# Where in a 256-byte block the operands of 17,664 matmuls begin: one offset for all activations, one for high weights, one for low weights

## The chip, the cores and the metric

The kernel runs on one core of a Trainium2 chip. The metric is the device time of one execution in microseconds (us); three runs of the kernel before took 2746.3, 2747.49 and 2748.06 us, so the median is 2747.49 us. Engines are called PE (TensorE), DVE (VectorE), ACT (ScalarE), POOL (GpSimd) and SP (SyncE).

## What is computed

One inference step of a decoder with two layers, on 256 prompt positions and 8 x 8 sample positions, 320 columns in all, with 2048 features. Layer 0 mixes tokens by gated linear attention, layer 1 by a gated MLP over chunks of 128 positions; each is followed by a dense MLP with a squared ReLU, and after each of the four there is a residual with a layer norm:

```python
for i in range(DEPTH):                       # DEPTH = 2, D_MODEL = 2048, D_FF = 8192
    if i % N_MIXERS == 0:
        h, s = gla_mixer(x, gla_w_in[j], gla_w_gate[j], gla_b_gate[j], gla_norm_g[j],
                         gla_w_out[j], gla_state0[j])
    else:
        h, v_rows = sg_mixer(x, sg_w_in[j], sg_b_in[j], ..., sg_w_out[j])
    x = layer_norm(DEEPNORM_ALPHA * x + h, ln1_g[i], ln1_b[i])
    x = layer_norm(DEEPNORM_ALPHA * x + sq_relu_mlp(x, mlp_w1[i], mlp_w2[i]), ln2_g[i], ln2_b[i])

def sq_relu_mlp(x, w1, w2):
    return jnp.square(jax.nn.relu(x @ w1)) @ w2
```

All inputs are float32. Nearly all of the work is the products with the weight matrices, some 400 MB that are read once.

## The kernel before

Features lie on the 128 partitions and positions along the free axis, so that an activation is 16 k tiles (`KT`) of 128 x 320 floats, 1280 bytes a tile and partition. Each float32 product is made of three products of a shorter float type (`F32R`): an activation is kept as a high part and a low part (`xh`, `xl`; `yh`, `yl`; `hh`, `hl`; `oh`, `ol`; `ph`, `pl`; `dgh`, `dgl`), and so are the weights (`wh`, `wl`).

**A unit.** `unit` (L117) loads one block of weights, 4 k tiles by 256 columns, 512 KB, from SP's queue into a `raw` buffer (three deep); ACT copies it to `wh` (L128), which rounds it, and DVE subtracts to get `wl` (L129). `group` (L143) then runs over the unit's two halves of 128 output features and its four k tiles, and `mm3` (L136) issues three matmuls, a triple, for each: 24 matmuls a unit.

```python
nc.tensor.matmul(ps, wl[:, kk, s], x_h, start=first, stop=False)
nc.tensor.matmul(ps, wh[:, kk, s], x_l, start=False, stop=False)
nc.tensor.matmul(ps, wh[:, kk, s], x_h, start=False, stop=last)
```

The weights are the stationary operand and the activations stream. PE loads the weights of the next matmul while the current one streams, so that a triple has these pairs side by side: `x_h` streams beside the load of `wh`, `x_l` beside a second load of the same `wh`, `x_h` beside the load of the next `wl`.

**The rings.** `wh` and `wl` have four buffers each in the pool `wa` (ring a). From the last part of the output projection of layer 0 on there is a second pool `wb` of the same size (ring b), and units alternate between the two (`next_ring`, L132). An order of the instructions is made by the tile framework's scheduler.

**The activations.** `bigtile` (L176) makes a tile of 16 x 322 floats; `TW` is 322 because a product of un-normed activations (`dgh`, `dgl`, `gemm_of`) has two more columns. `starts` puts an activation some floats further into its tile: `mlp` (L784) uses `8 * c` for chunk c of its four chunks, in layer 0 for both parts, in layer 1 for the low part alone, and `gemm_of` 32 for the high part of `y` in layer 1. One chunk of an MLP is 32 units on `y` (first product) and 32 units on `h` (second product); the first chunk's first product begins with 8 units of 322 columns.

The addresses of the built program, modulo 256 bytes, are these. A k tile is five blocks of 256 bytes (1280) long, and a step of `wh` or `wl` 512 or 1024 bytes, so that the offset is one for all 320-column matmuls of a tile. With 322 columns the step is 1288 bytes and the offset moves on by 8.

| stretch, us from the start | activations | high part at | low part at |
|---|---|---|---|
| to 1355, `x`, `o`, `y` of layer 0 | most units | 32 | 160 |
| 679.70 to 792.23, `h` chunk 0, layer 0 | 32 units | 32 | 160 |
| 904.76 to 1017.71, `h` chunk 1, layer 0 | 32 units | 64 | 192 |
| 1130.25 to 1242.67, `h` chunk 2, layer 0 | 32 units | 96 | 224 |
| 1355.20 to 1467.70, `h` chunk 3, layer 0 | 32 units | 128 | 0 |
| 1496 to 1824, `y`, `p` of the gated MLP | most units | 32 | 160 |
| 2049.88 to 2162.52 and other `y` chunks, layer 1 | 32 units each | 160 | 160 |
| 2162.52 to 2274.52, `h` chunk 1, layer 1 | 32 units | 32 | 192 |
| 2387.16 to 2499.90, `h` chunk 2, layer 1 | 32 units | 32 | 224 |
| 2612.54 on, `h` chunk 3, layer 1 | 32 units | 32 | 0 |

Weights of ring a begin at 160, high and low; those of ring b at 224, high and low.

**The heads.** In layer 0 the attention of head h is interleaved with the projections of the next (`Head.steps`). `sample_o` squares the sample outputs into `sq` (L571), a buffer of its own, and DVE reduces it to `s1` (L573), of which PE forms a sum (L576). `ev_k` of the next head writes two tiles `kend` (L371 and L372) in the ring `vfm`, two buffers of 1024 bytes, which PE transposes (L382).

Of the kernel before, what the change touches and what calls it, by code (L numbers as in the profile page):

```python
# [8 lines left out]
F32 = mybir.dt.float32  # L9
F32R = mybir.dt.float32r  # L10
# [5 lines left out]
P = 128  # L16
D = 2048
KT = D // P
TP = 256
DB, DS = 8, 8  # L20
T = TP + DB * DS
TW = T + 2
# [8 lines left out]
UK = 4  # L31
UN = 256
NU = KT // UK


V_BG, V_NG = 0, 8
# [5 lines left out]
class Ring:  # L42


    def __init__(self, pool, tag):
        self.pool, self.tag = pool, tag


class Side:
# [17 lines left out]
def step_kernel(ctx: ExitStack, tc: tile.TileContext, A):  # L67
# [3 lines left out]
    def nm(s):  # L71
        uid[0] += 1
        return f"{s}_{uid[0]}"


    cp = ctx.enter_context(tc.tile_pool(name="cp", bufs=1))
# [32 lines left out]
    nc.vector.memset(eps_l[:], LN_EPS)  # L109
    eps_h = cp.tile([P, 1], F32, tag="epsh", name="eps_h")  # L110
    nc.vector.memset(eps_h[:], HEAD_EPS)

    def col(c):
        return vec[:, c : c + 1]
# [2 lines left out]
    def unit(w, row0, q, col0, ring):  # L117

        raw = wraw.tile([P, UK, UN], F32, tag="raw", name=nm("raw"))
        src = w[row0 // (UK * P) + q, col0 // UN]  # L120
        hi = ring.pool.tile([P, UK, UN], F32R, tag="h" + ring.tag, name=nm("wh"))
        lo = ring.pool.tile([P, UK, UN], F32R, tag="l" + ring.tag, name=nm("wl"))
        units[0] += 1
        step = 2 if units[0] <= 2 else UK
        for k in range(0, UK, step):
            ks = slice(k, k + step)
            nc.sync.dma_start(raw[:, ks, :], src[:, ks, :])
            nc.scalar.copy(hi[:, ks, :], raw[:, ks, :])  # L128
            nc.vector.tensor_sub(lo[:, ks, :], raw[:, ks, :], hi[:, ks, :].bitcast(F32))  # L129
        return hi, lo  # L130
# [42 lines left out]
    w_in = A["gla_w_in"]  # L173
    C_Q, C_K, C_V, C_R = 0, H * DK, 2 * H * DK, 2 * H * DK + H * DV

    def bigtile(tag, dt, name, width=T, start=0):  # L176

        t = (lp if tag == "b1" else big).tile([P, KT * TW], dt, tag=tag, name=nm(name))
        return t[:, start : start + KT * width].rearrange("p (k t) -> p k t", t=width)

    def parts(pair, name, width=T, starts=(0, 0)):
        return (bigtile(pair + "0", F32R, name + "h", width, starts[0]),
                bigtile(pair + "1", F32R, name + "l", width, starts[1]))

    xh, xl = parts("a", "x")
    o_all = bigtile("b0", F32, "o_all")
# [106 lines left out]
    class Head:  # L293
# [266 lines left out]
        def sample_o(hd):  # L560
            h, s1 = hd.h, hd.s1
            os_ = gp.tile([P, DV], F32, tag="sq", name=nm("os"))
            nc.scalar.copy(os_[:], hd.po[:])
            pt = gltile()
            for vt in range(4):
                nc.tensor.transpose(pt[:, vt * P : (vt + 1) * P], os_[:, vt * P : (vt + 1) * P], ident[:])
            pv = pt[:].rearrange("p (v c t) -> p v c t", v=4, c=2)
            o_s = o_all[:, 4 * h : 4 * h + 4, TP:T]
            nc.scalar.copy(o_s, pv[:, :, 0, :])
            nc.vector.tensor_add(o_s, o_s, pv[:, :, 1, :])  # L570
            sq = gp.tile([P, 4, DB * DS], F32, tag="sqs", name=nm("sq"))  # L571
            nc.scalar.activation(sq[:], o_s, AF.Square)
            nc.vector.tensor_reduce(s1[:, TP:T], sq[:].rearrange("p v t -> p t v"), axis=AX.X, op=ALU.add)  # L573

            pr = gltile(T)
            nc.tensor.matmul(pr[:], ones[:], s1[:], start=True, stop=True)  # L576
            hd.rs = gp.tile([P, T], F32, tag="rs", name=nm("rs"))
            rsqrt(hd.rs[:], pr[:], 1.0 / DV, HEAD_EPS, eps_h, gp)
# [33 lines left out]
    def second_half():  # L612

        nonlocal lp, l2, z, gl, mx
        side.flush()
        split_o(range(4 * (H - 1), 4 * H))
        gst.close()
        gls.close()
        gl = ctx.enter_context(tc.tile_pool(name="gs", bufs=2, space=bass.MemoryType.PSUM))
        mx = ctx.enter_context(tc.tile_pool(name="mx", bufs=2, space=bass.MemoryType.PSUM))  # L620
        banks[0] = 3
        lp = ctx.enter_context(tc.tile_pool(name="lp", bufs=1))
        l2 = ctx.enter_context(tc.tile_pool(name="l2", bufs=2))
        wb = ctx.enter_context(tc.tile_pool(name="wb", bufs=4))
        rings.append(Ring(wb, "b"))
        z = lp.tile([P, KT, T], F32, tag="z", name="z")
        for q in range(2):
            nc.gpsimd.dma_start(z[:, 8 * q : 8 * q + 8, :], xT[:, 8 * q : 8 * q + 8, :])

# [118 lines left out]
                  lambda n, ps, i=i: evict(2 * i + n, ps), side, before=before if i == 0 else None)  # L748
            i += n2

    def gemm_of(norm, out, w, col0, evict_raw, evict, starts=(0, 0)):

        yh, yl = parts(out, "y", starts=starts)
        norm.close()
        side = Side([lambda j=j: norm.apply(j, yh, yl) for j in range(KT)], 3 * NU)
        group(w, 0, (col0, col0 + UN), *norm.raw, evict_raw, side, width=TW)
        side.flush()
        for i in range(2, D // UN):
            group(w, 0, (col0 + i * UN,), yh, yl, lambda n, ps, i=i: evict(2 * i + n, ps))
        return yh, yl  # L760
# [23 lines left out]
    def mlp(i, norm, y_in, h_in, vg, vb, raw, last=False):  # L784

        w1, w2 = A["mlp_w1"][i], A["mlp_w2"][i]
        NC_ = 4
        for c in range(NC_):
            hs = []

            def sq_relu(j, x, r):
                if not hs:
                    hs.extend(parts(h_in, "h", starts=(8 * c, 8 * c) if i == 0 else (0, 8 * c)))
                hh, hl = hs
                f = l2.tile([P, T], F32, tag="f", name=nm("f"))
                nc.vector.scalar_tensor_tensor(f[:], x, 0.0, r[:], op0=ALU.max, op1=ALU.mult)
                nc.scalar.copy(hh[:, j, 0:T], f[:])
                nc.vector.tensor_sub(hl[:, j, 0:T], f[:], hh[:, j, 0:T].bitcast(F32))

            def evict(j, ps):  # L800
                r = l2.tile([P, T], F32, tag="r", name=nm("r"))
                nc.scalar.activation(r[:], ps[:], AF.Relu)  # L802
                sq_relu(j, ps[:], r)

            def evict_raw(j, ps):
                t, wb_ = norm.correct(ps)
                r = l2.tile([P, T], F32, tag="r", name=nm("r"))
                nc.scalar.activation(r[:], t[:], AF.Relu, bias=wb_)
                sq_relu(j, r[:], r)

            if c == 0:
                yh, yl = gemm_of(norm, y_in, w1, 0, evict_raw, evict, starts=(0, 0) if i == 0 else (32, 0))
            else:
                gemm(w1, 0, c * D, yh, yl, evict)
            if c < NC_ - 1:
                def evz(j, ps, s=ALPHA if c == 0 else 1.0):
                    nc.vector.scalar_tensor_tensor(z[:, j, :], z[:, j, :], s, ps[:], op0=ALU.mult, op1=ALU.add)
                gemm(w2, c * D, 0, *hs, evz)
            else:
                return residual_gemm(w2, *hs, c * D, 1.0, vg, vb, raw, last=last)  # L820
# [209 lines left out]
```

## Time and profile before

| | us |
|---|---|
| median of three runs | 2747.49 |
| the profiled execution | 2747.28 |
| its span, first to last instruction | 2745.6 |
| PE matmul busy | 2726.5 |
| DVE busy | 1544.6 |
| ACT busy | 1182.2 |

The busy time of PE says little about its pace, since matmuls overlap and their ends are modelled: 309 ns is the mean of one, while a new one starts every 147 ns or so. So a stretch is read here by its length and the work in it: windows of the trace begin and end at the start of the first matmul of a unit. A window counts one to three matmuls more than its own, those still under way at its edges.

### The profile page before, as it was taken

The page shows a single profiled execution, that of the slowest core. Times are in us where ns is not written, and L with a number is a line of the kernel's source. Part 1 is how long each engine was busy: PE and PEld are TensorE (multiplying, and loading weights), DVE is VectorE, ACT ScalarE, POOL GpSimd, SP SyncE. Part 2 cuts the span into 40 slices and gives each one's busy share as a digit, 9 for nine tenths or more (in the row PEclk, how much of TensorE's full clock was granted, in tenths as well). Part 3 has the DMA queues.
Part 4 walks back from the last instruction along what each step waited for, and adds up shares of the span by engine and source line. Part 5 has one row for each costly group of instructions (what it writes and reads, how often), then busy time and mean ns, then how long its engine had stood idle before and what let it go on. Part 6 is the DMA issues. An engine that isn't in the chain of part 4 may idle for free.

```text
span 2745.6 us, 44621 instructions
## 1 busy us (share of the span) xinstructions
PE 2726.5 (99%) x18493; PEld 2703.0 (98%) x18493; DVE 1544.6 (56%) x2284; ACT 1182.2 (43%) x1698; POOL 54.4 (2%) x84
## 2 busy tenths in 40 slices
PE   8999999999999999999999999999999999999998
PEld 8999999999999999999999999999999999999998
DVE  6577577885444434444468774686444444444446
ACT  5545455464334334323345554455334333323433
POOL 1000000000000000000001000000000000000001
PEclk9999999999999999999999999999999999999999
DMA  6557566644444444444445444454444444444442
GB/s 224 178 191 237 163 209 212 208 145 154 152 148 153 147 150 150 152 148 150 150 146 169 148 138 130 141 160 154 147 153 147 153 149 151 149 151 149 151 148 75
DMA packets 126395, 434.51 MB, mean 158 GB/s; under 512 B 13680, under 2 KB 17904, under 8 KB 126192
## 3 DMA queue, kind: packets, MB, share of 16 engines
q1 hardware_dynamic: 118800, 407.29, 47.4%
q0 software_dynamic: 6512, 23.20, 2.4%
q8 instruction: 144, 2.36, 0.4%
q10 hardware_dynamic: 880, 1.18, 0.1%
q14 instruction: 59, 0.48, 0.1%
HBM read 409.60 MB, written 22.02 MB: 157 GB/s over the span
## 4 chain that ended last, share of the span: by engine, by line
PE 98%; DVE 1%; ACT 1%; DMA 0%; issue 0%; SPq 0%; ACTq 0%; DVEq 0%
PE mm L139 31%; PE mm L141 31%; PE mm L140 31%; PE gl L551 1%; PE gl L554 1%; PE gl L509 1%; DMA xr<-xT 0%; PE gl L889 0%; PE gl L493 0%; ACT z L963 0%; PE gl L884 0%; PE gl L494 0%; PE gl L418 0%; PE gl L420 0%; PE gl L472 0%
## 5 line engine op out<-in xcount | busy, mean ns | idle before, releaser
L129 DVE TENSOR_TENSOR wl<-raw,wh 128x1024 fp32r<-128x1024 f32 (+1 forms) x738 | 900.9, 1222 | 966.2 <-ACT wh L128 963.7
L128 ACT CAST wh<-raw 128x1024 fp32r<-128x1024 f32 (+1 forms) x738 | 771.0, 1046 | 1235.4 <-PE mm L141 1120.1
L141 PE MATMUL mm<-yh,wh 128*128 128x320 f32 x2368 | 730.9, 309 | 0.0
L140 PE MATMUL mm<-yl,wh 128*128 128x320 f32 x2368 | 728.5, 308 | 0.0
L139 PE MATMUL mm<-yh,wl 128*128 128x320 f32 x2368 | 725.5, 309 | 0.0
L141 PE MATMUL mm<-hh,wh 128*128 128x320 f32 x2048 | 632.2, 309 | 0.0
L139 PE MATMUL mm<-hh,wl 128*128 128x320 f32 x2048 | 631.8, 309 | 0.0
L140 PE MATMUL mm<-hl,wh 128*128 128x320 f32 x2048 | 631.4, 308 | 0.0
L140 PEld LDWEIGHTS mm<-yl,wh 128*128 128x128 f32 x2368 | 444.8, 188 | 0.0
L141 PEld LDWEIGHTS mm<-yh,wh 128*128 128x128 f32 x2368 | 444.0, 188 | 0.0
L139 PEld LDWEIGHTS mm<-yh,wl 128*128 128x128 f32 x2368 | 443.0, 188 | 0.0
L139 PEld LDWEIGHTS mm<-hh,wl 128*128 128x128 f32 x2048 | 385.0, 188 | 0.0
L140 PEld LDWEIGHTS mm<-hl,wh 128*128 128x128 f32 x2048 | 384.5, 188 | 0.0
L141 PEld LDWEIGHTS mm<-hh,wh 128*128 128x128 f32 x2048 | 384.3, 188 | 0.0
L139 PE MATMUL mm<-xh,wl 128*128 128x320 f32 x768 | 242.1, 316 | 8.7 <-ACT xh L202 5.6
L140 PE MATMUL mm<-xl,wh 128*128 128x320 f32 x768 | 240.8, 314 | 0.0
L141 PE MATMUL mm<-xh,wh 128*128 128x320 f32 x768 | 239.2, 311 | 0.0
L139 PEld LDWEIGHTS mm<-xh,wl 128*128 128x128 f32 x768 | 145.8, 190 | 13.6 <-ACT xh L202 5.6
L140 PEld LDWEIGHTS mm<-xl,wh 128*128 128x128 f32 x768 | 145.8, 190 | 3.5 <-issue 1.2
L141 PEld LDWEIGHTS mm<-xh,wh 128*128 128x128 f32 x768 | 145.9, 190 | 1.3
L139 PE MATMUL mm<-ph,wl 128*128 128x320 f32 x256 | 78.6, 309 | 1.0 <-ACT ph L922 1.0
L802 ACT ACTIVATE r<-mm 128x320 f32<-128x320 f32 x120 | 52.5, 438 | 62.1 <-PE mm L141 62.1
(271 smaller groups left out, 2490.2 us busy)
## 6 DMA issues: line engine op xcount, KB each, us to landing
raw<-mlp_w SPq DMA_DIRECT2D x512, 512.0 KB, 3.5
raw<-gla_w_in SPq DMA_DIRECT2D x94, 512.0 KB, 3.8
raw<-sg_w_in SPq DMA_DIRECT2D x64, 512.0 KB, 3.6
st<-state SPq DMA_DIRECT2D x32, 512.0 KB, 4.2
o_state_s<-st POOLq DMA_DIRECT2D x32, 512.0 KB, 4.1
raw<-gla_w_out SPq DMA_DIRECT2D x32, 512.0 KB, 3.7
raw<-sg_w_out SPq DMA_DIRECT2D x32, 512.0 KB, 3.6
z<-xT POOLq DMA_DIRECT2D x2, 1280.0 KB, 11.3
```

What stands on the lines that cost most here:

```text
L128: nc.scalar.copy(hi[:, ks, :], raw[:, ks, :])
L129: nc.vector.tensor_sub(lo[:, ks, :], raw[:, ks, :], hi[:, ks, :].bitcast(F32))
L139: nc.tensor.matmul(ps, wl[:, kk, s], x_h, start=first, stop=False)
L140: nc.tensor.matmul(ps, wh[:, kk, s], x_l, start=False, stop=False)
L141: nc.tensor.matmul(ps, wh[:, kk, s], x_h, start=False, stop=last)
L509: nc.tensor.matmul(pu[:], hd.ktp[:, blk, kt * P : (kt + 1) * P], hd.vtp[:, blk, :], start=(blk == 0), stop=(blk == 1))
L551: nc.tensor.matmul(po[:], qm[:, kt, b * P : (b + 1) * P], part[:], start=False, stop=(b == DB - 1 and kt == 1 and part is sth))
L554: nc.tensor.matmul(pu[:], kz[:, g, i, kt * P : (kt + 1) * P], hd.vts[:, g, :], start=True, stop=True)
L802: nc.scalar.activation(r[:], ps[:], AF.Relu)
```

## The change

All tiles of activations grow to `BIG` = 16 x 320 + 64 floats, a multiple of 256 bytes, and begin at a multiple of 256. Activations of 320 columns begin 32 floats (128 bytes) into the tile, those of 322 columns at its beginning; `starts` is gone. Padding tiles (`fill`, `gap`, `fill_b`, `fill_l`), which no instruction uses, shift what follows them: `wh` begins at 0 in both rings, and since `gap` lies between the high and the low buffers, `wl` begins at 64 in both. To make room `sq` of `sample_o` moves into the ring `vfm`. In the built program every main matmul of 320 columns has its activations at 128, `wh` at 0 and `wl` at 64.

```diff
+LINE = 64
+BIG = KT * T + LINE
...
-        self.pool, self.tag = pool, tag
+        self.pool, self.tag, self.gap = pool, tag, False
+
+    def part(self, p, name):
+
+        t = self.pool.tile([P, UK, UN], F32R, tag=p + self.tag, name=name)
+        if not self.gap:
+            self.pool.tile([P, LINE // 4], F32, tag="gap", name=name + "_gap", bufs=1)
+            self.gap = True
+        return t
...
+    cp.tile([P, LINE - 8], F32, tag="fill", name="fill")
...
-        hi = ring.pool.tile([P, UK, UN], F32R, tag="h" + ring.tag, name=nm("wh"))
-        lo = ring.pool.tile([P, UK, UN], F32R, tag="l" + ring.tag, name=nm("wl"))
+        hi = ring.part("h", nm("wh"))
+        lo = ring.part("l", nm("wl"))
...
-    def bigtile(tag, dt, name, width=T, start=0):
-
-        t = (lp if tag == "b1" else big).tile([P, KT * TW], dt, tag=tag, name=nm(name))
+    def bigtile(tag, dt, name, width=T):
+        t = (lp if tag == "b1" else big).tile([P, BIG], dt, tag=tag, name=nm(name))
+        start = LINE // 2 if width == T else 0
         return t[:, start : start + KT * width].rearrange("p (k t) -> p k t", t=width)
...
-            sq = gp.tile([P, 4, DB * DS], F32, tag="sqs", name=nm("sq"))
+            sq = g2.tile([P, 4, DB * DS], F32, tag="vfm", name=nm("sq"))
...
+        wb.tile([P, LINE // 4], F32, tag="fill", name="fill_b", bufs=1)
         z = lp.tile([P, KT, T], F32, tag="z", name="z")
+        lp.tile([P, 3 * LINE // 4], F32, tag="fill", name="fill_l")
...
-                    hs.extend(parts(h_in, "h", starts=(8 * c, 8 * c) if i == 0 else (0, 8 * c)))
+                    hs.extend(parts(h_in, "h"))
...
-                yh, yl = gemm_of(norm, y_in, w1, 0, evict_raw, evict, starts=(0, 0) if i == 0 else (32, 0))
+                yh, yl = gemm_of(norm, y_in, w1, 0, evict_raw, evict)
```

The instructions are the same in kind and number, and SP's and POOL's queues keep their order. DVE's, ACT's and PE's change only around the place where a head ends and the next begins, three times.

DVE's queue there, before. `kend_1693` is the second of the next head, `s_132_1012` is `s1`, `sq_1583` the squares, `o_all` the outputs, which are weighted:

```order
L129 TENSOR_TENSOR wl_1782<-raw_1780,wh_1781 128x1024
L372 TENSOR_TENSOR kend_1693<-kte_1667,fac 128x256
L378 TENSOR_TENSOR kst_1695<-kte_1667,kst_1695 128x8x16
L397 SCALAR_TENSOR_TENSOR qd_1664<-mm_1278,eb_1311 128x320
L573 TENSOR_REDUCE s_132_1012<-sq_1583 128x64
```

The same place of DVE's queue after the change, where `kend_1677` is the first `kend` of the head, which stood six rows earlier, and `kend_1695` the second:

```order
L386 TENSOR_TENSOR kend_1677<-kte_1669,fac 128x256
L392 TENSOR_TENSOR kst_1697<-kte_1669,kst_1697 128x8x16
L411 SCALAR_TENSOR_TENSOR qd_1666<-mm_1280,eb_1313 128x320
L587 TENSOR_REDUCE s_132_1014<-sq_1585 128x64
L471 SCALAR_TENSOR_TENSOR o_all_91<-o_all_91,vec,sr_1075 128x320
L471 SCALAR_TENSOR_TENSOR o_all_91<-o_all_91,vec,sr_1077 128x320
L471 SCALAR_TENSOR_TENSOR o_all_91<-o_all_91,vec,sr_1274 128x320
L471 SCALAR_TENSOR_TENSOR o_all_91<-o_all_91,vec,sr_1276 128x320
L411 SCALAR_TENSOR_TENSOR qd_1666<-mm_1281,eb_1319 128x320
L414 TENSOR_TENSOR qx_1667<-qd_1666,fac 128x192
L414 TENSOR_TENSOR qx_1667<-qd_1666,fac 128x128
L386 TENSOR_TENSOR kend_1695<-kte_1669,fac 128x256
```

The second `kend` moved behind the reduction, four weightings and the two `qx`.

PE's queue at the same place, before; `mm_1718` is an output of the next projection, `ident` the matrix for transposes:

```order
L139 MATMUL mm_1718<-xh_88,wl_1752 128x320
L140 MATMUL mm_1718<-xl_89,wh_1751 128x320
L141 MATMUL mm_1718<-xh_88,wh_1751 128x320
L576 MATMUL gl_1586<-s_132_1012,ones 128x320
L382 MATMUL gl_1680<-ident,kend_1675 128x128 x2
L384 MATMUL gl_1680<-ident,kst_1677 128x128 x2
L382 MATMUL gl_1698<-ident,kend_1693 128x128 x2
L384 MATMUL gl_1698<-ident,kst_1695 128x128 x2
```

PE's queue after:

```order
L151 MATMUL mm_1720<-xl_90,wh_1753 128x320
L152 MATMUL mm_1720<-xh_89,wh_1753 128x320
L590 MATMUL gl_1588<-s_132_1014,ones 128x320
L396 MATMUL gl_1682<-ident,kend_1677 128x128 x2
L398 MATMUL gl_1682<-ident,kst_1679 128x128 x2
L150 MATMUL mm_1720<-xh_89,wl_1754 128x320
...
L152 MATMUL mm_1721<-xh_89,wh_1753 128x320
L396 MATMUL gl_1700<-ident,kend_1695 128x128 x2
L398 MATMUL gl_1700<-ident,kst_1697 128x128 x2
```

The sum over `s1` and the first transposes come one triple earlier among the main matmuls, and the second transposes some triples later.

## Rows read from the trace of the kernel before

**Rows 1.** The page: span, busy time with its share of each engine, granted clock.

```profile
span 2745.6 us, 44621 instructions
...
PE 2726.5 (99%) x18493; PEld 2703.0 (98%) x18493; DVE 1544.6 (56%) x2284; ACT 1182.2 (43%) x1698; POOL 54.4 (2%) x84
...
PEclk9999999999999999999999999999999999999999
```

**Rows 2.** Waits of PE: waiter <- releaser: us in all, times, longest us.

```profile
PE mm L139 <- ACT xh L202: 5.6, 1, 5.6
PE mm L139 <- DVE qd L397: 2.1, 1, 2.1
```

**Rows 3.** Groups: line, engine, op, count; busy us, mean ns; idle before, releasers.

```profile
L128 ACT CAST wh<-raw 128x1024 fp32r<-128x1024 f32 (+1 forms) x738 | 771.0, 1046 | 1235.4 <-PE mm L141 1120.1 <-issue 38.2 <-DMA raw<-gla_w_out 24.0
...
L141 PE MATMUL mm<-dgh,wh 128*128 128x322 f32 x192 | 59.6, 310 | 0.0
```

**Rows 4.** Windows of 32 units: from:to us, length, PE busy (matmuls), clock, DMA, GB/s.

```profile
679.70:792.23 112.53, 112.53 (x770) 1.00 0.48 150
904.76:1017.71 112.95, 112.95 (x770) 1.00 0.48 150
2049.88:2162.52 112.64, 112.64 (x771) 1.00 0.49 150
2162.52:2274.52 112.00, 112.00 (x771) 1.00 0.48 151
2387.16:2499.90 112.74, 112.74 (x770) 1.00 0.47 150
```

**Rows 5.** Windows of single units with weights of ring a.

```profile
823.88:827.40 3.52, 3.52 (x27) 1.00 0.49 156
2306.20:2309.72 3.52, 3.52 (x26) 1.00 0.42 151
2194.02:2197.52 3.50, 3.50 (x27) 1.00 0.47 151
2425.96:2429.44 3.48, 3.48 (x27) 1.00 0.37 148
2418.86:2422.38 3.52, 3.52 (x26) 1.00 0.47 149
2651.23:2654.75 3.52, 3.52 (x26) 1.00 0.51 150
2644.21:2647.72 3.51, 3.51 (x27) 1.00 0.45 149
1386.80:1390.30 3.50, 3.50 (x27) 1.00 0.50 154
```

**Rows 6.** Windows of single units with weights of ring b.

```profile
820.37:823.88 3.51, 3.51 (x27) 1.00 0.52 149
2302.68:2306.20 3.52, 3.52 (x26) 1.00 0.43 149
2190.52:2194.02 3.50, 3.50 (x27) 1.00 0.50 150
2422.38:2425.96 3.58, 3.58 (x27) 1.00 0.42 148
2415.34:2418.86 3.52, 3.52 (x26) 1.00 0.50 150
2647.72:2651.23 3.51, 3.51 (x26) 1.00 0.50 152
2640.68:2644.21 3.53, 3.53 (x27) 1.00 0.50 149
933.00:936.53 3.53, 3.53 (x26) 1.00 0.51 149
1158.35:1161.87 3.52, 3.52 (x26) 1.00 0.51 151
```

**Rows 7.** Timeline where a head ends: start us, length us, engine, line, operation.

```profile
155.86 0.61 DVE L573 TENSOR_REDUCE s<-sq 128x64 f32<-128x256 f32 x1
...
159.58 0.70 PE L576 MATMUL gl<-s,ones 128*128 128x320 f32 x2
```

More of the change, by code (lines that the diff above doesn't have):

```diff
@@ L174, in step_kernel, with parts @@
     C_Q, C_K, C_V, C_R = 0, H * DK, 2 * H * DK, 2 * H * DK + H * DV
-    def bigtile(tag, dt, name, width=T, start=0):
-        t = (lp if tag == "b1" else big).tile([P, KT * TW], dt, tag=tag, name=nm(name))
+    def bigtile(tag, dt, name, width=T):
+        t = (lp if tag == "b1" else big).tile([P, BIG], dt, tag=tag, name=nm(name))
+        start = LINE // 2 if width == T else 0
         return t[:, start : start + KT * width].rearrange("p (k t) -> p k t", t=width)
-    def parts(pair, name, width=T, starts=(0, 0)):
-        return (bigtile(pair + "0", F32R, name + "h", width, starts[0]),
-                bigtile(pair + "1", F32R, name + "l", width, starts[1]))
+    def parts(pair, name, width=T):
+        return bigtile(pair + "0", F32R, name + "h", width), bigtile(pair + "1", F32R, name + "l", width)
     xh, xl = parts("a", "x")
@@ L749, in gemm, with gemm_of @@
             i += n2
-    def gemm_of(norm, out, w, col0, evict_raw, evict, starts=(0, 0)):
-        yh, yl = parts(out, "y", starts=starts)
+    def gemm_of(norm, out, w, col0, evict_raw, evict):
+        yh, yl = parts(out, "y")
         norm.close()
```

## The prediction

> **What bounds the kernel now.** [...] Then the list of who waits for whom on PE [rows 2]: its longest entry is 5.6 us, once, at the start, and the second is 2.1 us, once. Nothing that ScalarE, VectorE or the DMA queues do in the main loops ends a wait of PE. So the time is the number of matmuls times the distance between their starts, and only what changes that distance can move it.
>
> The work comes in units: one unit is one 512 KB block of weights, split by one ScalarE copy, and 24 matmuls on it. The copy line counts 738 [rows 3]; the first two units copy in two halves, so there are 736 units. The matmuls of one of three products on 322 columns count 192 [rows 3], which is 24 units of 8; the other 712 units work on 320 columns. [...]
>
> [...] The blocks of [rows 4] do the same 768 matmuls at the same clock, and differ by 0.95 us. What differs is where the operands begin in a 256-byte block. I write hi/lo for the distance in bytes, modulo 256, by which the high and the low activations begin past the weights of that unit. [rows 5] has units of ring a, [rows 6] of ring b, in the order 32/160, 160/160, 32/192, 32/224 (two), 32/0 (two) of activation offsets, with 128/0 at the end of ring a and 64/192 and 96/224 at the end of ring b. Less the ring's 160 or 224 this gives:
>
> - lo at 0 past the weights: 128/0 3.52 (ring a) and 3.52 (ring b), 0/0 3.52, 64/0 3.58 and 3.52.
> - hi at 128 or 64 past them and lo elsewhere: 128/32 3.50, 128/64 3.48 and 3.52, 128/96 3.52 and 3.51, 64/192 3.51, 64/224 3.50, 64/32 3.51 and 3.53.
> - others: 192/192 3.52, 224/96 3.50, 96/224 3.53.
>
> Two things are seen. The same difference gives the same time in both rings where both have it (128/0: 3.52 and 3.52), so the difference counts more than the place. And no placement that occurs falls below 3.48 or above 3.58.
>
> **The change part by part.** *Placement of the 712 units.* After the change both rings have the same relations: the first two matmuls of a triple run with high and low activations 128 past the high weights, and the third (high activations on high weights) runs while low weights are loaded, 64 before the activations. So hi is at 128 and at 64, lo at 128. The trace has hi at 128 and at 64 often, lo at 128 never. The nearest rows are the second group above: averaged by layout, 3.50, (3.48 + 3.52) / 2 = 3.50, (3.52 + 3.51) / 2 = 3.515, 3.51, 3.50 and (3.51 + 3.53) / 2 = 3.52, their mean is 3.508. The layout most units have now is 32/160, 112.53 / 32 = 3.517 [rows 4]. That is 9 ns less for a unit, 712 x 0.009 = 6.4 us. The ends are the fastest and the slowest unit of the trace, 3.48 and 3.58: 26 us less and 45 us more. I take 3.508, since its rows share two of the three relations; the ends are single units whose neighbours cancel them (3.48 stands beside 3.58 in one block of 112.74 us, [rows 4]).
>
> The rows show that the time of a unit depends on placement. [...]
>
> *The 24 units of 322 columns.* Their k tiles lie 1288 bytes apart, so that their place in a block moves by 8 bytes each time, before and after; only the first place changes. I take 0; the spread of [rows 5] and [rows 6], 0.10 us, bounds it by 24 x 0.10 = 2.4 us either way.
>
> *The new sharing of two buffers.* The squares of the sample outputs move from a buffer of their own into the ring of `vfm`, two deep, that `kend` also uses. So the two `kend` of the next head wait for a buffer. The order shows where they go: on VectorE the first falls back by six rows and the second by ten, from ahead of the reduction of the squares to behind it, and in PE's queue the transposes that read the second come behind 12 more matmuls, in each of three heads. The reduction begins at 155.86 and lasts 0.61 us; PE reaches the product that needs it at 159.58 [rows 7]. In the new order PE reaches it three matmuls earlier, 0.44 us, still 2.7 us after the reduction ended. Queued behind the waiting `kend` on VectorE are the next split of weights and the low part of `qm`; the weights are needed only after the units that PE still has in its ring of four. I take 0; if that cover were gone it would cost the 0.42 us of one `kend` three times, 1.3 us.
>
> *All else.* The same instructions in the same number; the queues of SyncE and GpSimd keep their order row for row. Tiles of 512-column products and vectors in the heads also move to other offsets; PE waits there at single points only [rows 2] and I take 0, with 1 us either way. Padding tiles cost no instruction.
>
> The sum: the profiled execution took 2747.28 us, 1.7 more than its span, and is 0.2 us under the median of 2747.49. 2747.3 - 6.4 = 2740.9, so 2741 us.
>
> **The rivals.**
> *The locked case: no change.* Where high and low activations begin at the same offset, ring a at 0/0 and ring b at 192/192 both take 3.52 us, and the block is 112.64 [rows 4]: there the weights' place seems not to matter. The change makes high and low equal everywhere. Then a unit takes 3.52: 712 x 0.003 = 2 us more, 2749 us. Against it: in those rows high and low weights are also at one offset, which the change ends. A change that does nothing to placement is excluded: in the built program all of the matmuls of the main loop have the new offsets.
>
> *Slower: the low activations meet the weight load.* Lo at 128 past the weights never occurred, and lo is what decides the slow rows: with hi at 64, lo 224 gives 3.50 and lo 0 gives 3.52 to 3.58 [rows 6]. If lo at 128 is such a place, the second matmul of each triple, whose companion is a second load of the same high weights, is slowed in all 712 units. The price is that of the slowest layout, (3.58 + 3.52) / 2 = 3.55: 712 x 0.033 = 23 us, 2771; at the next slowest, 3.53 (96/224), it is 9 us, 2756. It decides from a unit of 3.525 on. For it: with hi at 128, lo at 96, the nearest to 128 that occurs, gives 3.52 and 3.51, more than lo at 32 or 64. Against it: five of nine layouts with lo elsewhere than 0 are at or below 3.51.
>
> [...]
>
> **How the numbers follow.** Forecast, a little faster, 3.49 to 3.513 us a unit (2728 to 2744): 0.42. Locked, within 2744 to 2753: 0.27. Slower, 2753 to 2771: 0.22. Much faster, below 2728: 0.09, of which 0.02 for a collapse of the excess. A measurement of this kernel can tell about 0.2%, 5.5 us, from no change: 2742.0 to 2753.0. Of the forecast's own range 2742 to 2744 falls inside it, some 0.05. So faster 0.46, within 0.32, slower 0.22. The range of 8 in 10 leaves out the lower half of the much faster case with its tail and the upper part of the slower: 2718 to 2760. The forecast's own range is 2728 to 2744.
>
> **What would show each step.** In the profile after, PE must again have no wait of more than some us. Blocks of the main loops should all be alike to 0.1 us, since they now have one layout: near 112.2 for the forecast (32 x 3.508), 112.6 for the locked case, 113.0 or more for the slower one. Units of ring a and ring b should take the same. If blocks of one layout differed from each other, the tiles' places beyond 256 bytes would count too, and averaging by layout was wrong. The forecast fails if lo at 128 has a time of its own that none of the rows foretells.

## The result and the profile after

The kernel after the change takes **2715.18 us** (median of four runs, 2714.76 to 2715.70), beside 2747.77 us for the kernel before (four runs, 2746.30 to 2748.36): a ratio of **0.9882, 95% interval 0.9865 to 0.9899**, 32.6 us less. The forecast was 2741 us with a range down to 2718: the sign was right, the size was not, and the time lies just below the range.

The page of the kernel after, answering to [rows 1]: span, busy time of the engines, granted clock.

```profile
span 2713.2 us, 44623 instructions
...
PE 2692.2 (99%) x18493; PEld 2668.4 (98%) x18493; DVE 1543.0 (57%) x2284; ACT 1183.7 (44%) x1698; POOL 54.8 (2%) x84
...
PEclk9999999999999999999999999999999999999999
```

PE is still what bounds the kernel, at the same clock (0.999 in the mean before and after). Its busy time falls by 34.3 us, the span by 32.4; the other 1.9 us are more idle time. The waits of PE after the change, answering to [rows 2] (waiter <- releaser: us in all, times, longest us):

```profile
PE mm L150 <- ACT xh L216: 5.7, 1, 5.7
PE mm L150 <- DVE wl L140: 2.2, 2, 1.6
PE mm L150 <- DVE qd L411: 2.2, 1, 2.2
```

The first and third are those of before; the second had 0.9 us in the kernel before, and its longest, 1.6 us, lies at the start. So the gain isn't a wait that went away. It is pace. Windows of 32 units in the kernel after (from:to us, length, PE busy and matmuls, clock, DMA share, GB/s); but for the fourth, a `y` chunk, they are the `h` chunks 0, 1, 2 of layer 0 and 1, 2 of layer 1, answering to [rows 4]:

```profile
675.05:785.98 110.93, 110.93 (x770) 1.00 0.49 152
896.92:1007.85 110.93, 110.93 (x770) 1.00 0.47 152
1118.78:1229.72 110.94, 110.94 (x771) 1.00 0.48 152
2027.09:2138.02 110.93, 110.93 (x770) 1.00 0.48 152
2138.02:2248.95 110.93, 110.93 (x770) 1.00 0.50 152
2359.89:2470.82 110.93, 110.93 (x770) 1.00 0.49 152
```

Blocks that took 112.00 to 112.95 us now all take 110.93 or 110.94: 3.467 us a unit, in both rings. A unit of ring b and the one of ring a behind it, answering to [rows 5, 6]:

```profile
910.78:914.25 3.47, 3.47 (x26) 1.00 0.47 156
914.25:917.72 3.47, 3.47 (x27) 1.00 0.43 151
```

Which of the three matmuls of a triple became shorter is seen in the groups (line, engine, operation, shapes, count; busy us, mean ns). Busy times of overlapping matmuls can't be added up to a time, but they can be compared with each other. Those of `y`, before and then after:

```profile
L141 PE MATMUL mm<-yh,wh 128*128 128x320 f32 x2368 | 730.9, 309 | 0.0
L140 PE MATMUL mm<-yl,wh 128*128 128x320 f32 x2368 | 728.5, 308 | 0.0
L139 PE MATMUL mm<-yh,wl 128*128 128x320 f32 x2368 | 725.5, 309 | 0.0
```

```profile
L152 PE MATMUL mm<-yh,wh 128*128 128x320 f32 x2368 | 726.4, 307 | 0.0
L150 PE MATMUL mm<-yh,wl 128*128 128x320 f32 x2368 | 724.3, 309 | 0.0
L151 PE MATMUL mm<-yl,wh 128*128 128x320 f32 x2368 | 716.7, 303 | 0.0
```

Before, all three had 308 or 309. It is above all the second, the low activations on the high weights (L140 before, L151 after), that is shorter. The start times of the same records say it more sharply. Averaged over the triples of 320 columns that run on undisturbed (no other product and no wait in them), the distances from each of the three starts to the next were 146.7, 145.9 and 147.0 ns before, 439.6 together, and are 147.5, 140.2 and 145.8 ns after, 433.5 together; eight triples are a unit. Such averages of start-to-start distances, by ring and layout, are what the experiments below are read by, beside the windows; there they leave out the last triple of each unit, behind which the other ring follows.

**Where the 32 us are.** The mean unit of 320 columns went from 3.518 to 3.468 us: 712 x 0.050 = 35.6 us. The 24 units of 322 columns went from 3.559 to 3.547, 0.3 us. Back came 1.9 us of idle time and some 1.6 us elsewhere, mostly in the heads. One head of layer 0 with its 24 units, first in the kernel before, then after:

```profile
110.07:218.69 108.62, 108.62 (x720) 1.00 0.61 199
```

```profile
109.73:217.68 107.95, 107.95 (x720) 1.00 0.60 200
```

It gained 0.67 us where 24 x 0.05 = 1.2 were due. The small products don't hold the rest: in these two windows the distances that begin at one of them add up to 0.08 us less than before. Those that begin at a second matmul of a triple add up to 1.02 us less and at a third to 0.16 less, but those at a first to 0.58 us more. Why the first ones lose here wasn't followed further.

### The profile page after: what moved, and what is told of

It reads as the page before. It is cut to its first block, busy times and chain, and to the rows that moved or that the text cites. A ratio compares the mean times of both kernels' runs of the same rounds, so it can differ in the third digit from the quotient of the medians.

```text
span 2713.2 us, 44623 instructions
## 1 busy us (share of the span) xinstructions
PE 2692.2 (99%) x18493; PEld 2668.4 (98%) x18493; DVE 1543.0 (57%) x2284; ACT 1183.7 (44%) x1698; POOL 54.8 (2%) x84
## 4 chain that ended last, share of the span: by engine, by line
PE 98%; DVE 1%; ACT 0%; DMA 0%; issue 0%; SPq 0%; ACTq 0%; DVEq 0%
PE mm L150 32%; PE mm L152 31%; PE mm L151 31%; PE gl L565 1%; PE gl L568 1%; PE gl L523 1%; PE gl L905 0%; DMA xr<-xT 0%; PE gl L507 0%; ACT z L979 0%; DMA raw<-gla_w_in 0%; PE gl L900 0%; PE gl L508 0%; PE gl L432 0%; PE gl L434 0%
## 5 line engine op out<-in xcount | busy, mean ns | idle before, releaser
L140 DVE TENSOR_TENSOR wl<-raw,wh 128x1024 fp32r<-128x1024 f32 (+1 forms) x738 | 902.1, 1223 | 943.4 <-ACT wh L139 941.6
L151 PE MATMUL mm<-yl,wh 128*128 128x320 f32 x2368 | 716.7, 303 | 0.0
L151 PE MATMUL mm<-hl,wh 128*128 128x320 f32 x2048 | 619.6, 303 | 0.0
L151 PEld LDWEIGHTS mm<-yl,wh 128*128 128x128 f32 x2368 | 444.4, 188 | 0.0
L151 PEld LDWEIGHTS mm<-hl,wh 128*128 128x128 f32 x2048 | 384.4, 188 | 0.0
L151 PE MATMUL mm<-xl,wh 128*128 128x320 f32 x768 | 236.4, 308 | 0.0
L150 PEld LDWEIGHTS mm<-xh,wl 128*128 128x128 f32 x768 | 145.2, 189 | 15.0 <-ACT xh L216 5.7
L151 PEld LDWEIGHTS mm<-xl,wh 128*128 128x128 f32 x768 | 145.4, 189 | 3.6 <-issue 1.2
L814 DVE TENSOR_TENSOR hl<-f,hh 128x320 fp32r<-128x320 f32 x128 | 62.3, 489 | 29.5 <-ACT hh L813 29.5
```

## The experiments

All offsets below are modulo 256 bytes. The **step** is how far the low weights begin past the high ones: 0 before, 64 after. The **place** hi/lo is how far the high and the low activations begin past the high weights, as in the prediction; after the change it is 128/128 in both rings. Experiments on layouts compute the same in the same instructions; only padding and starts differ. Times are of one run each, beside a run of the kernel before on the same chip: 2746.49 us for the first four, 2747.59 for the next four, 2745.81 for the four after, 2746.20 for the last two (by the numbers in their names, e1 to e14). The diffs are cut to the lines that matter; `...` marks what is left out, among it padding that keeps the activations in place.

### One part of the change undone

`e1_gap0` takes the step away and keeps the activations at 128/128; `e3_act0` keeps the step and puts all activations at 0/0; `e4_before_gap` is the kernel before with nothing but the step; `e2_gap192` has a step of 192 for 64.

```diff
 e1_gap0
-        if not self.gap:
-            self.pool.tile([P, LINE // 4], F32, tag="gap", name=name + "_gap", bufs=1)
-            self.gap = True
...
 e3_act0
...
-        return bigtile(pair + "0", F32R, name + "h", width), bigtile(pair + "1", F32R, name + "l", width)
+        return (bigtile(pair + "0", F32R, name + "h", width, 0),
+                bigtile(pair + "1", F32R, name + "l", width, 0))
 e4_before_gap (kernel before)
...
+            self.pool.tile([P, 16], F32, tag="gap", name=name + "_gap", bufs=1)
...
 e2_gap192
-            self.pool.tile([P, LINE // 4], F32, tag="gap", name=name + "_gap", bufs=1)
+            self.pool.tile([P, 48], F32, tag="gap", name=name + "_gap", bufs=1)
...
```

> The changed kernel without its quarter block between the weights: activations at 128, high and low weights both at 0, in both rings. Step theory (the quarter block from low to high weights shortens one matmul of each triple): the gain goes, units of 3.52 us as in the blocks of before with equal offsets, 2748 to 2752 us. Place theory (the low activations, 128 past the high weights, are what is fast): the low weights don't matter, units stay at 3.467 us, 2715 us.

> The changed kernel with all activations at 0 in place of 128, high weights at 0, low weights at 64. Step theory: activations only have to be equal, units of 3.467 us, 2715 us. Place theory: the low activations begin where the high weights begin, which was the slow place before (3.52 to 3.58 us), units of 3.52 us or more, 2750 us or more.

> The kernel before with one thing of the change, a quarter block between high and low weights (low at 224 in ring a, at 32 in ring b); its many activation offsets stay. Step theory: the blocks with equal activations (160 and 160) fall from 3.52 to 3.467 us a unit; the others move by some 0.05 us either way; 2720 to 2740 us. Place theory: the matmuls beside loads of high weights keep their places, units stay near 3.517 us, 2745 to 2750 us.

> The changed kernel with low weights three quarters of a block after the high ones (192) in place of one quarter, which is one quarter before them; activations at 128. Step theory: a step of a quarter either way is still a step, units of 3.45 to 3.49 us, 2705 to 2730 us; if only the direction of the change is good, 3.52 us and 2750 us. Place theory: 3.467 us, 2715 us.

| kernel | step | place hi/lo | us | block of 32 units |
|---|---|---|---|---|
| after | 64 | 128/128 | 2715.18 | 110.93 |
| `e1_gap0` | 0 | 128/128 | 2748.67 | 112.64 |
| `e3_act0` | 64 | 0/0 | 2748.22 | 112.64 |
| `e4_before_gap` | 64 | as before | 2753.72 | 112.31 to 113.54 |
| `e2_gap192` | 192 | 128/128 | 2777.3 | 114.34 |

The same window, `h` chunk 0 of layer 0, in `e1_gap0`, then in `e3_act0`:

```profile
680.21:792.85 112.64, 112.64 (x770) 1.00 0.49 150
```

```profile
679.35:791.99 112.64, 112.64 (x771) 1.00 0.48 150
```

Each part alone is worth nothing: with either undone the block is at 112.64, 3.520 us a unit, which is the locked case of the prediction to the digit. The step alone, given to the kernel before, leaves its blocks unequal and on the whole no shorter. So the gain belongs to the combination. A step with the same distance the other way (192) is a loss of 1.1%.

`e2_gap192` shows one thing more. It has a single layout, but two paces. Four single units of its `h` chunk 3 in layer 0: the first, the last of a run up to 1428.87, the next from 1432.55, the last:

```profile
1368.13:1371.70 3.57, 3.57 (x27) 1.00 0.42 138
1425.30:1428.87 3.57, 3.57 (x26) 1.00 0.52 146
1432.55:1436.07 3.52, 3.52 (x26) 1.00 0.41 130
1478.31:1481.83 3.52, 3.52 (x26) 1.00 0.50 149
```

The timeline between them (start us, length us, engine, line, operation) has one thing that the units before and after don't have, a single matmul of another kind (L721, a sum for the layer norm) between two of a triple:

```profile
1429.32 0.31 PE L150 MATMUL mm<-hh,wl 128*128 128x320 f32 x1
1429.47 0.31 PE L721 MATMUL gl<-a,ones_r 128*128 128x320 f32 x1
1429.62 0.31 PE L151 MATMUL mm<-hl,wh 128*128 128x320 f32 x1
```

From there the same work on the same addresses runs at 3.520 instead of 3.573, to the end of the chunk. It isn't the only place. This sum stands between two matmuls of a triple at five times of the run. The first, at 515.17 us, meets a pace of 440.0 ns a triple and leaves it there. The other four, at 1429.47, 1547.98, 1787.52 and 2701.81 us, have 446.6 to 446.8 ns a triple before them and 439.8 to 440.1 behind them. The units around the last one:

```profile
2697.65:2701.22 3.57, 3.57 (x27) 1.00 0.51 149
2704.90:2708.42 3.52, 3.52 (x27) 1.00 0.38 144
```

In between the slow pace is back, and the MLP blocks there are at 114.34; what brings it back wasn't followed. In the kernel after and in `e1_gap0` the same sum changes the pace by no more than 0.2 ns. So the pace isn't a function of the addresses alone: in this layout the stream keeps one of two rhythms from unit to unit until something comes between. That the sum is what turns it is read from its place, four times of four; the kernel wasn't run without it. In these loops the paces are also stepped: a triple is 433.3 ns (110.93 / 256), 440.0 (112.64 / 256) or 446.7 (by the distances), some 6.7 ns apart each time.

### Place or difference

`e5_map64` shifts all weights of ring b by 96 bytes, keeps a step of 64 in both rings, and puts the eight `h` chunks, high and low alike, at eight offsets.

```diff
+AT = (((0, 0), (16, 16), (32, 32), (48, 48)), ((8, 8), (24, 24), (40, 40), (56, 56)))
...
-                    hs.extend(parts(h_in, "h"))
+                    hs.extend(parts(h_in, "h", at=AT[i][c]))
...
-        wb.tile([P, LINE // 4], F32, tag="fill", name="fill_b", bufs=1)
+        wb.tile([P, 40], F32, tag="fill", name="fill_b", bufs=1)
```

> The changed kernel with two things of placement altered: all weights of ring b lie 96 bytes further (high at 96, low at 160), and the h activations of the eight MLP chunks begin at 0, 64, 128, 192 (layer 0) and 32, 96, 160, 224 (layer 1), high and low alike. Difference theory (only the distances from weights to activations count): a unit of ring b takes what a unit of ring a takes at the same distance; the distance of 128 gives 3.467 us in ring a (chunk at 128) and in ring b (chunk at 224), a distance of 0 gives 3.52 in both. Block theory (operands have to begin at the middle and the beginning of a block): ring b is at 3.52 us everywhere, also with the chunk at 224.

It took 2738.81 us. Units of this kernel: the first two, of `h` chunk 2 in layer 0, activations at 128, in ring b and then in ring a; the other two, of the last chunk, activations at 224, in ring b and then in ring a:

```profile
1140.11:1143.63 3.52, 3.52 (x27) 1.00 0.48 149
1143.63:1147.11 3.48, 3.48 (x27) 1.00 0.48 151
2618.60:2622.07 3.47, 3.47 (x27) 1.00 0.47 146
2622.07:2625.60 3.53, 3.53 (x27) 1.00 0.51 150
```

The short unit is in ring a where the activations are at 128 and in ring b where they are at 224: both times 128 past the high weights. The distances of its triple in ring b, 147.4, 140.4 and 145.9 ns, are those of the kernel after. At the seven other differences the two rings agree too, five of them to 0.6 ns and at worst to 3.2 (a triple of 440.0 in both at 0/0, 435.8 and 435.9 at 64/64, 440.1 and 439.9 at 192/192, 443.0 and 446.2 at 160/160). So the differences count, and not the place in the block as far as these eight go. The short unit of ring a is 3.480 here and not 3.467: it loses 13 ns where its neighbour has another layout. That this is the rhythm of `e2_gap192` again is likely, not shown.

### How narrow the place is

`e7_uneq` and `e12_uneq64` put the high and the low part of `h` at different offsets; the weights stay as after the change, but for a step of 0 in ring b of `e7_uneq`. `e10_fine` moves `h` by 4 to 16 bytes; in ring b it was meant to have a step of 80, and the program as built has 96. `e6_map128_192`, `e9_map96_32` and `e14_map160_224` are `e5_map64` with the steps of their names in ring a and ring b; in the last the low part came to lie 128 from the high one in four of the eight chunks.

```diff
 e7_uneq (hi, lo of the eight chunks, in floats)
+AT = (((32, 0), (32, 16), (32, 48), (0, 32)), ((16, 32), (48, 32), (32, 24), (32, 40)))
 e12_uneq64
+AT = (((32, 16), (16, 32), (16, 16), (32, 24)), ((16, 0), (40, 32), (32, 8), (24, 32)))
 e10_fine
+AT = (((28, 28), (30, 30), (31, 31), (33, 33)), ((34, 34), (36, 36), (29, 29), (35, 35)))
...
+            n = {"a": 16, "b": 20}[self.tag]
...
 e6_map128_192; e9_map96_32; e14_map160_224 (step in floats)
+            n = {"a": 32, "b": 48}[self.tag]
+            n = {"a": 24, "b": 8}[self.tag]
+            n = {"a": 40, "b": 56}[self.tag]
```

> The changed kernel with no quarter block in ring b (low weights at 0 too), one in ring a, and the h activations of the eight chunks at high/low 128/0, 128/64, 128/192, 0/128, 64/128, 192/128, 128/96, 128/160. If the shortened matmul is the one of the low activations because these lie 128 from the high weights: 0/128, 64/128 and 192/128 keep a short second product (140 ns) in ring a. If it is the equal place of all activations that lets the gain stand: every unequal pair is above 3.49 us. Ring b without the step: 3.50 to 3.55 us throughout.

> The changed kernel with h activations of the eight chunks at high/low 128/64, 64/128, 64/64, 128/96, 64/0, 160/128, 128/32, 96/128, weights as in the change in both rings. If only equal places 128 past the high weights are fast: no chunk under 3.467 us, 64/64 at 3.49 us. If a better place is to be had with unequal parts: a chunk under 3.46 us, most likely 128/64, of which single triples were far below the others.

> The changed kernel with low weights 80 bytes after the high ones in ring b (64 in ring a as before), and the h activations of the eight chunks at 112, 120, 124, 132, 136, 144, 116, 140, high and low alike: a few bytes beside the middle. If the place is 32 bytes wide or more: units of ring a stay at 3.467 to 3.48 us. If it is narrow: 3.50 us and more within 16 bytes, and offsets that are no multiple of 16 are slower still, as the products of 322 columns are (3.55 us).

> The changed kernel with low weights 128 after the high ones in ring a and 192 in ring b, and the h activations of the eight chunks at 0, 64, 128, 192, 32, 96, 160, 224, high and low alike. If the fast place needs a quarter step exactly: no unit under 3.50 us. If a triple is fast wherever two of its three distances are 128 apart in some order: some chunks near 3.467 us, above all where the activations lie 192 or 64 from the high weights. Ring b with the chunk at 128 repeats the 3.564 us of the run with 192.

> The changed kernel with low weights 96 bytes after the high ones in ring a and 32 in ring b, h activations of the eight chunks at 0, 64, 128, 192, 32, 96, 160, 224, high and low alike. If the fast place is a single one: no unit under 3.48 us. If it is a valley around a step of 64: the chunk at 128 is at about 3.49 us in both rings.

> Low weights 160 bytes after the high ones in ring a and 224 (32 before them) in ring b, the eight parts h of the MLPs with high and low activations together at eight places 32 bytes apart. Theory (only few sets of differences are fast): nearly all triples 438 to 446 ns, at most one of the sixteen at 433 to 434, the kernel at 2743 to 2760 us. Rival (with the right step a triple can fall below 433 ns, so that the change stopped short of the best place): some of the sixteen below 430 ns.

They took 2738.09 us (`e7_uneq`), 2728.76 (`e12_uneq64`), 2743.87 (`e10_fine`), 2748.31 (`e6_map128_192`), 2749.87 (`e9_map96_32`) and 2750.88 (`e14_map160_224`). In `e12_uneq64` both rings are alike, so a block has one layout; its blocks at 128/64, 64/128, 64/64 and 160/128:

```profile
675.06:786.86 111.80, 111.80 (x770) 1.00 0.50 151
897.80:1010.09 112.29, 112.29 (x771) 1.00 0.49 151
1121.04:1232.54 111.50, 111.50 (x770) 1.00 0.49 152
2143.44:2256.93 113.49, 113.49 (x770) 1.00 0.48 149
```

None of its eight layouts reaches 110.93; in the seven unequal ones the second matmul of the triple takes 144 to 149 ns, not 140. So at this step the gain is gone in every unequal layout that was tried. In `e10_fine`, ring a has 434.3 ns a triple with activations at 128, 436.9 at 124, 443.3 at 120, 453.0 at 116, and 450.7 at 132; its block at 116:

```profile
2381.48:2497.47 115.99, 115.99 (x771) 1.00 0.47 146
```

The place is not the same width on both sides: four bytes short of it cost 2.6 ns a triple, four bytes past it 16.4. There, at 132, a unit of ring a takes 3.61 us, more than the slowest of the rows of before (3.58):

```profile
1359.70:1363.31 3.61, 3.61 (x26) 1.00 0.57 151
```

In all of these ring b has a step of 96, so each is seen beside a neighbour in another layout. Steps of 96, 128, 160, 192 and 224 have nothing below 435.6 ns. One layout was a surprise. In `e9_map96_32`, ring b has a step of 32, and with activations at 64/64 (`h` chunk 1 of layer 0) its units took 3.47 us beside units of ring a at 3.52:

```profile
919.76:923.23 3.47, 3.47 (x26) 1.00 0.47 149
923.23:926.75 3.52, 3.52 (x27) 1.00 0.49 149
```

There the triple is 141.8, 148.2 and 143.3 ns: the short ones are the first and the third, and the sum, 433.4, is that of the change.

### The whole kernel at the second place

```diff
-            self.pool.tile([P, LINE // 4], F32, tag="gap", name=name + "_gap", bufs=1)
+            self.pool.tile([P, LINE // 8], F32, tag="gap", name=name + "_gap", bufs=1)
...
-        start = LINE // 2 if width == T else 0
+        start = LINE // 4 if width == T else 0
```

> Both rings with the low weights 32 bytes after the high ones and all activations of 320 columns at 64: the layout whose units of ring b took 3.468 us in the map with steps 96 and 32, beside units of ring a at 3.519. Theory (the pace is set by the differences, and more than one set of differences gives the short triple): both rings at 3.467 to 3.47 us a unit, the kernel at 2713 to 2719 us. Rival (the layout changed holds the only fast place, and the short units of that map were borrowed from the state left by their neighbours): units at 3.50 to 3.55, the kernel at 2735 to 2775 us.

It took 2714.45 us, 0.7 less than the kernel after, which one run can't tell from the same. Its block and its groups:

```profile
674.43:785.36 110.93, 110.93 (x770) 1.00 0.49 152
```

```profile
L151 PE MATMUL mm<-yl,wh 128*128 128x320 f32 x2368 | 733.3, 310 | 0.0
L152 PE MATMUL mm<-yh,wh 128*128 128x320 f32 x2368 | 724.1, 306 | 0.0
L150 PE MATMUL mm<-yh,wl 128*128 128x320 f32 x2368 | 715.5, 305 | 0.0
```

The same 110.93, got in another way: here the second matmul is the longest, in the kernel after the shortest. So a gain of this size doesn't need the low activations to be 128 past the high weights; there are at least two layouts in which a triple locks at 433.3 ns, and among some fifty with high and low activations together, over the eight steps from 0 to 224, none has less. Most of these were seen only beside a ring of another layout, where the place of the change itself shows up to 434.8. In both layouts that lock at 433.3 ns the low weights begin halfway between the high weights and the activations (64 of 128, 32 of 64). That isn't enough: a step of 96 with activations at 192 has 439.6 ns, beside a ring of another layout.

### What the distance hangs on

`e8_sizes` asks whether the distance from one matmul to the next hangs on the weight load or on the columns. Ring a has no step, ring b one of 64. In seven of the eight second products of the MLPs it leaves out part of the work: it uses fewer columns, or fewer output features and so a smaller load of weights, or both, for all but the first and the last triple of each sum.

```diff
+MODES = (((128, 320), (64, 320), (128, 256), (32, 320)), ((128, 192), (96, 320), (128, 128), (64, 256)))
...
+        m, c = (P, cn) if first or last or mode[0] == (P, T) else mode[0]
+        s = slice(n * P, n * P + m)
+        ps, x_h, x_l = ps[0:m, 0:c], x_h[:, 0:c], x_l[:, 0:c]
```

> The changed kernel without the quarter block in ring a and with it in ring b; in the second product of seven of the eight MLP chunks all triples but the first and the last of each sum are cut: weights of 64 of 128 output features (chunk 1, layer 0), of 32 (chunk 3, layer 0), of 96 (chunk 1, layer 1); 256 of 320 columns (chunk 2, layer 0), 192 (chunk 0, layer 1), 128 (chunk 2, layer 1); both 64 features and 256 columns (chunk 3, layer 1). The rest of those products is left out. [...]

It took 2650.17 us. Windows of 23 matmul distances of one size in ring a: 320 columns with 128, 64, 96 and 32 features, then 128 features with 256, 192 and 128 columns:

```profile
681.41:684.78 3.37, 3.37 (x26) 1.00 0.48 156
905.02:908.36 3.34, 3.34 (x25) 1.00 0.48 157
2114.47:2117.84 3.37, 3.37 (x25) 1.00 0.51 158
1333.96:1337.32 3.36, 3.36 (x25) 1.00 0.48 156
1128.38:1131.10 2.72, 2.72 (x25) 1.00 0.61 175
1912.92:1915.49 2.57, 2.57 (x26) 1.00 0.48 137
2338.11:2340.68 2.57, 2.57 (x26) 1.00 0.46 137
```

Divided by 23 that is 146.5, 145.2, 146.5 and 146.1 ns for 320 columns with 128, 64, 96 and 32 features: a quarter of the weights saves next to nothing. 256 columns take 118.3 ns; 192 and 128 columns both take 111.7. So the distance doesn't shrink with the weight load. With the columns it shrinks only so far: four fifths of 146.5 would be 117.2 at 256 columns, 1.1 ns less than measured, but three fifths would be 87.9 at 192, where 111.7 was measured. In ring b, which has the layout of the change, the short second matmul of 140.0 ns is gone when the load has fewer features (146.1 to 146.7), and the triple takes 436.9 to 440.0 ns in place of 433.3: the good place holds for full loads only.

One rival is settled by the traces: that PE is held up by what other engines or transfers do in the same memory. In the MLPs of the kernel after, the triples during which ACT, DVE and POOL all stood still average 433.3 ns (266 of them), those that their work covers from end to end 433.3 too (1651), and those without a DMA packet under way 433.3 as well (430). In `e1_gap0` each of these groups has 440.0.

### The other edit

`e11_sq_own` is the kernel after with the squares in a buffer of their own again.

```diff
-            sq = g2.tile([P, 4, DB * DS], F32, tag="vfm", name=nm("sq"))
+            sq = gp.tile([P, 4, DB * DS], F32, tag="sqs", name=nm("sq"))
```

> The changed kernel with the squares back in a buffer of their own: kend no longer waits for it. By the prediction this term is nothing, 2715 us within 1.3 us. The rival: the later transposes cost PE some 0.4 us a head, then 2713 us and the stretch of each head's end is shorter.

It took 2715.01 us, against 2715.18: nothing that one run can tell. In the kernel after the reduction and PE's product on it, answering to [rows 7], stand here:

```profile
155.06 0.62 DVE L587 TENSOR_REDUCE s<-sq 128x64 f32<-128x256 f32 x1
```

```profile
158.55 0.70 PE L590 MATMUL gl<-s,ones 128*128 128x320 f32 x2
```

From the end of the reduction to the product it is 2.87 us, close to the 2.7 that were foreseen as cover.

## Why the prediction was right and wrong

**Right: what bounds the kernel, and by what it could change.** PE is bound by the pace of its matmuls before and after, no long wait came or went (the longest is 5.6 us before, 5.7 after), and the pace moved with the offsets. That the difference counts and not the place was read from two rows (128/0 at 3.52 in both rings); `e5_map64` showed it at eight differences. Both things that the prediction asked of the trace were seen: blocks alike to 0.01 us, and ring a like ring b. That the sign came out right is in part luck: the rows behind it don't contain the new layout, and of three layouts that differ from it in one part `e1_gap0` and `e3_act0` gain nothing and `e2_gap192` loses.

**Wrong: the size of the one term that mattered, the placement of the 712 units.** It was set at 6.4 us and measured 35.6. The step that failed is the average. Six layouts were averaged to 3.508 us a unit, "since its rows share two of the three relations", as though each relation added its own part. That reading was wrong too: each of the six has only one of the three. 128/32, 128/64 and 128/96 have the high activations 128 past the high weights, 64/192, 64/224 and 64/32 have them 64 past the low ones, and none has the low activations at 128. And the runs show that the relations don't add. `e1_gap0` has two of them, all but the 64 from the low weights, and takes 3.520, no gain at all; the blocks of `e12_uneq64` with the high part alone at 128 have two others and take 3.49 to 3.55; with all three it is 3.467, less than any of the six. A mean over neighbours can't show such a place, and `e10_fine` shows how little neighbours tell: 4 bytes past it a triple takes 450.7 ns for 434.3.

**Wrong with it: the end of the range.** The fastest unit of the trace, 3.48, was taken as the end and as cancelled by its neighbour of 3.58. It was rather a hint: its layout, 128/64 with a step of 0, whose units of before took 3.48 to 3.52, has a triple of 435.6 ns, 3.485 us a unit, in ring b of `e7_uneq`, beside other neighbours. And it was no floor, since no layout of that trace had more than one of the relations. The case "much faster", below 2728 us, is what came, and it got 0.09; the fast end, 26 us less for a unit of 3.48, was nearly the right price for the measured 32.6. How large the "excess" is whose collapse got 0.02 of that, no run shows, since none shows what a matmul would take for its columns alone; what the runs showed is 433.3 ns a triple, 3.467 us a unit, as the least of any loop on 320 columns.

**The rivals.** The locked case is real and not of this kernel: `e1_gap0` and `e3_act0` are it, at 3.520. The slower case did not come. Its thought, that low activations at 128 may have a time that none of the rows foretells, came true the other way round and only in company: with the two other relations the second matmul of a triple takes 140 ns in place of 146, while `e1_gap0`, with the low activations at 128 as well, has 146.6.

**What the layouts move.** The layouts alone move the kernel from 2714.45 to 2777.3 us (`e13_place32`, `e2_gap192`) at equal work and an equal clock (0.999 and 1.000). So the pace hangs on how the addresses of the two operands lie to each other, as the rows of before had it (112.00 against 112.95 us for equal blocks). What in the chip makes it so, the runs do not say.

**The small terms.** The 322-column units, set at 0 within 2.4 us, gave 0.3. The shared ring, set at 0, gave nothing that a run can tell. "All else" was bounded by 1 us either way and came to some 3.5 us of loss: 1.9 of idle time, mostly at the start, and some 1.6 elsewhere, mostly in the heads.

**What stays open.** Why some differences take 6.7 ns off a triple of 440.0 and others add 6.7, why 192 and 128 columns take the same 111.7 ns, and by what the rhythm is kept from one unit to the next, no run here settles. Nothing below 433.3 ns was found, but most unequal layouts at steps other than 0 and 64, and steps that aren't multiples of 32, weren't tried.

## What to carry to other kernels

When PE is bound by its own pace and equal blocks take unequal times at an equal clock, tabulate the time against the differences of the operands' start addresses modulo 256, and then run the candidate layouts with the whole loop in one layout: padding adds no instruction, and here it was worth 1.2%. Don't average layouts, and don't take the fastest unit of a mixed loop as the floor, since its neighbours can hold it up (3.480 for 3.467 in `e5_map64`); put the low weights, the high weights and both activations in one fixed relation in every ring, and measure two or three of these. Recheck after any change of tile sizes, since 4 bytes the wrong way are enough to lose it (450.7 ns a triple in `e10_fine`).

## What was not expected of the hardware

- A matmul of a float32 product in three short ones takes 146.7 ns for 320 columns (a third of the 440.0 of `e1_gap0`) and 118.3 for 256 (`e8_sizes`), 0.46 ns a column both times, at a granted clock of 1.00; a smaller load of weights changes the 320 columns by 1.3 ns at most; at 192 and 128 columns both take 111.7 ns with full loads.
- Loops of one layout lock at 433.3, 440.0 or 446.7 ns a triple in six kernels here (others, as in `e12_uneq64`, lie between), and the pace has a memory: in `e2_gap192` it went from 3.573 to 3.520 us a unit at each of the four places where a single matmul from elsewhere met the slow pace, and in the `h` chunks it stayed there to the end.
- Two layouts reach the same 433.3 ns with different matmuls of the triple shortened, 147.5, 140.2, 145.8 (the kernel after) and 141.9, 148.3, 143.4 ns (`e13_place32`).
